# A hybrid decoder step: residual copy behind the token scaling, softmax bias from a minimum, sample probabilities a slot later

## The chip, the cores and the metric

The kernel runs on one core of one Trainium2 chip. The metric is the device time of one execution in microseconds (us); three runs are given, and their median is the time. One more execution was taken by the hardware profiler, and the rows of the profile come from it. Engines are named as the profile names them: PE is TensorE (matrix products and transposes), DVE is VectorE, ACT is ScalarE, POOL is GpSimd, SP is SyncE, which only issues transfers here.

## The reference

One layer of a decoder over a prompt of 1024 tokens and a sample group of 8 tokens (width 1024) that share the weights. A combined projection `w_in` feeds three mixers, whose outputs are gated, summed and merged; a SwiGLU follows. Cut to what the change touches:

```python
xn = rmsnorm(x, norm_mix_w)                       # the opening
sc_b, sc_c, sc_x, z, xbc, dt_raw, q, gates = split(xn @ w_in)
...
# mixer C: 4 heads of width 256 attend to 256 memory tokens
scores = einsum('blhd,bmhd->bhlm', q, mem_k) * (256 ** -0.5)     # 1/16
probs  = softmax(scores, axis=-1)
y_c    = einsum('bhlm,bmhd->blhd', probs, mem_v) @ w_attn_o
...
x = x + merge(...)          # the residual needs x as well as xn
x = x + swiglu(rmsnorm(x))
```

The prompt's memory keys and values are computed from `mem_prompt`; those of the sample tokens come from a cache.

## The kernel before

All matrix products run as split products: each fp32 operand is cut into a hi part (a cast) and a lo part (the remainder), and three products hi·hi, lo·hi and hi·lo are summed. Tensors lie with features on the 128 partitions and tokens along the free axis; the 1032 tokens are the prompt's 1024 and the 8 of the sample. A tile framework allots the buffers, and its scheduler settles the order of the instructions on each engine from the order of the program, from buffers and from estimated durations, so that a moved line can move others.

The stages by time in the profile: the opening (0 to 65 us), the in-projection by Strassen products, the state-space scan with the q projection as filler between the chunks, the attention (about 1340 to 1580 us) in between the out-projections, the merge and the SwiGLU, and the last rows.

**The opening** goes by four groups g of 256 tokens (the last with 8 more). For each group the rows of x are squared and summed (`square`, L528, ACT) and turned into reciprocal roots (`rsqrt`, `root_of`; L99 to L104), which PE spreads over the partitions (tile `ps_rb`) and DVE copies to `rbc`. Then `tokens(g, ks)` takes two of the eight feature blocks k at a time (one at a time in the last group): PE transposes x into one PSUM bank `ps_xt` (L495); ACT copies the bank to `xt` (L513) and starts the transfer of it to memory as `xT_d`, the residual kept for later (L515, on ACT's own queue); and `to_xn` makes the normalised tokens for each block: DVE multiplies the bank by the weight and `rbc` into `xw` (L501), ACT casts the hi part `xnh` (L502), DVE subtracts for the lo part `xnl` (L503). The pool of these banks, shared by all small PSUM tiles, has two buffers. Between the tiles of group g PE makes the first two products (`first_products`, tiles `ps_B` and `ps_C`, L565 to L567) and the step sizes (`step_sizes`, `ps_dt`, L575, L581) of group g - 1. Casts of the weights for the gemms that follow (`wz0h` by ACT, L152, `wz0l` by DVE, L153) stand among this work.

**The q projection**: `q_step` evicts each of eight blocks of q from PSUM by an ACT copy (L805), GpSimd copies the 8 sample columns to `qs`, and the block is stored to `q_d`.

**The attention** is cut into `pieces`, a list of slots each of which holds a few function calls; a pacing counter runs a slot or two after each of the out-projection's gemm steps. For each head h and each pair l2 of 128-token blocks, `a_scores` (L1647 to L1649, tile `psa`) makes the scores, `softmax` the probabilities: DVE takes the maximum (L1564) and multiplies it by -1/16 (L1565), ACT takes exp(score/16 + bias) with the sum (L1567), and DVE divides (L1571, L1573). `a_probs` (tile `psp`) transposes them and splits them, `a_out` (tile `psv`, copy to `ot` L1682) multiplies by the values. The sample tokens have pieces of their own: `s_query`, `s_keys`, `s_scores` (products of `qs` with the cached keys on DVE), then the list `late`: `s_softmax`, `s_values` (loads of cached values `vc`), `s_probs` (transposes into `pss_pT`, L1592), eight times `s_out` (`pso`, L1605), `s_back`. The weights `wo22r` and others are split among these pieces (L152, L153).

Of the kernel before, what the change touches and what calls it, by code (L numbers as in the profile page):

```python
# [11 lines left out]
AF = mybir.ActivationFunctionType  # L12
ALU = mybir.AluOpType
AX = mybir.AxisListType
# [12 lines left out]
KD = D // P  # L27
EPS = 1e-6
LAG = 3
GROUPS = 4  # L30
HEADS = 32
HPG = 8
# [9 lines left out]
def tile_kernel(ctx: ExitStack, tc, a, o):  # L42
    nc = tc.nc
    V, S, G, PE, SY = nc.vector, nc.scalar, nc.gpsimd, nc.tensor, nc.sync

    def f32(t):
        return t.bitcast(F32)
# [13 lines left out]
    def mm_ps(name):  # L61
        return pmm[0].tile([P, NCH, 512], F32, tag="mm", name=name)

    def sm_ps(name):
        return psm.tile([P, 512], F32, tag="sm", name=name)

    def dram(name, shape):
        return dp.tile(shape, F32, tag=name, name=name)
# [4 lines left out]
    def flat(ps):  # L73
        return ps[:, :, :CW]

    def t3(t, lo=0):
        return t[:, lo : lo + TT].rearrange("p (n c) -> p n c", n=NCH)
# [78 lines left out]
    def ev_tile(name, shape=(P, TT + 4), dt=F32):  # L156
        return ev.tile(list(shape), dt, tag="ev", name=name)
# [26 lines left out]
    def gemm(w, acts, name, width=P, off=0):  # L184

        hi, lo = w
        ps = mm_ps(name)
        nk = len(acts)
        n = int(pace[0] + pace[1])
        pace[1] += pace[0] - n  # L190
        marks = [nk * i // n for i in range(n)]
        between = seam.pop() if seam else None
        for k, (ah, al) in enumerate(acts):
            if between is not None:
                between(k)
            if k == 1 and owed:
                owed.pop()()
            for _ in range(marks.count(k)):
                tick()
            ks = slice(k * width + off, k * width + off + P)  # L200
            for i, (wt, x) in enumerate(((hi, ah), (hi, al), (lo, ah))):
                for n in range(NCH):
                    PE.matmul(  # L203
                        ps[:, n, :CW], wt[:, ks], x[:, n * CW : (n + 1) * CW],
                        start=(k == 0 and i == 0), stop=(k == nk - 1 and i == 2),
                    )
        return ps

    def wblock(w, col):
        return w[:, col : col + P].rearrange("(k p) c -> p k c", p=P)  # L210
# [10 lines left out]
    def b3(t, n):  # L221
        return t.rearrange("p (a b) -> p a b", a=n)

    def h3(t):
        return t.rearrange("p (n c) -> p n c", n=2)
# [16 lines left out]
    def st_ps(tag, name):  # L242
        return pst[0].tile([P, 2, 512], F32, tag=tag, name=name)
# [153 lines left out]
    v_d = dram("v_d", [2, P, D])  # L397
    ac_d = dram("ac_d", [GROUPS, NCK, HPG, P])
    ea_d = dram("ea_d", [GROUPS, NCK, HPG, P])
    bc_d = dram("bc_d", [GROUPS, NS, 2, P])  # L400
    qs_d = dram("qs_d", [NS, D])
# [21 lines left out]
    with tc.tile_pool(name="p0", bufs=1) as p0:  # L423
# [20 lines left out]
        ps = sm_ps("ps_mix")  # L444
# [26 lines left out]
        def par(key, i):  # L471
            return prm[:, PC[key] + i : PC[key] + i + 1]

        bias = cn.tile([P, 1], F32, tag="bias", name="bias")
# [14 lines left out]
        def part(g):  # L489
            c0, n = parts[g]  # L490
            return slice(c0, c0 + n)

        def turn(g, ps, at, of):
            for i, (t, n) in enumerate(srcs[g]):
                PE.transpose(ps[:, at + i * P : at + i * P + n], of(i, t, n), ident[:n, :n])  # L495

        def to_xn(g, k, ps):
            hi, lo = xn[k]
            c = part(g)
            xc = xw[k][:, c]  # L500
            first = V.scalar_tensor_tensor(xc, ps, par("mix", k), rbc[:, c], op0=ALU.mult, op1=ALU.mult)  # L501
            ins = S.copy(hi[:, c], xc)  # L502
            V.tensor_sub(lo[:, c], xc, f32(hi)[:, c])  # L503
            return ins.ins, first.ins

        def tokens(g, ks):

            n = parts[g][1]
            ps = sm_ps(f"ps_xt{g}{ks[0]}")
            for i, k in enumerate(ks):  # L510
                turn(g, ps, i * n, lambda _, t, m: t[:, k * P : (k + 1) * P])
            xt = p0.tile([P, 512], F32, tag="xt", bufs=4, name=f"xt{g}{ks[0]}")
            S.copy(xt[:, : len(ks) * n], ps[:, : len(ks) * n])  # L513
            to = xT_d[ks[0] :: 4] if len(ks) > 1 else xT_d[ks[0] : ks[0] + 1]
            S.dma_start(to[:, :, part(g)].rearrange("k p t -> p k t"), b3(xt[:, : len(ks) * n], len(ks)))  # L515
            for i, k in enumerate(ks):
                ins = to_xn(g, k, ps[:, i * n : (i + 1) * n])
            return ins

        def square(g, i):  # L520
# [119 lines left out]
    ys = cn.tile([P, 16, NS], F32, tag="ys", name="ys")  # L640
    bcs = ch.tile([P, GROUPS, NS, 2], F32, tag="bcs", name="bcs")

# [17 lines left out]
    def dt_tiles():  # L660
        mx, u, z, z2, q = (pd_.tile([P, W], F32, tag=n, name=n) for n in ("mx", "u", "z", "z2", "q"))
        da = pd_.tile([P, 9, HEADS], F32, tag="da", name="da")
        ach = pd_.tile([P, NCK, HEADS], F32, tag="ach", name="ach")
        return mx, u, z, z2, q, da, ach
# [33 lines left out]
    def dt_rows():  # L698
        act_, eat_ = (pd_.tile([HEADS, T], F32, tag="wide", bufs=2, name=n) for n in ("acT", "eaT"))

        V.tensor_copy(
            ach.rearrange("p c (g w t) -> p (c g) w t", g=GROUPS, w=2),
            acum.rearrange("p c (g t w) -> p (c g) w t", g=GROUPS, w=2),
        )
# [36 lines left out]
    def proj(col, name):  # L741
        return gemm(weights(wblock(w_in, col), "w" + name), xn, "ps_" + name)
# [58 lines left out]
    def q_step(i):  # L801
        def s():
            ps = proj(C_Q + i * P, f"q{i}")
            t = ev_tile(f"q{i}")
            S.copy(t3(t), flat(ps))  # L805
            G.tensor_copy(qs[:, i, :], t[:, T:TT])
            S.dma_start(q_d[i], t[:, :TT])

        return [Step(wblock(w_in, C_Q + i * P), f"wq{i}", s)]
# [523 lines left out]
    mx, u, z, z2, q, da, ach = dt_tiles()  # L1333
# [126 lines left out]
    ins = ((sc_d, a["w_sc_out"][0]), (yb_d, a["w_ssm_out"][0, 0:D]), (yb_d[8:16], a["w_ssm_out"][0, D : 2 * D]), (at_d, None))  # L1460
# [56 lines left out]
    if True:  # L1517
# [40 lines left out]
                    )  # L1558

        def softmax(pr, src, n, npart, name):  # L1560
            mxs = at.tile([P, 4], F32, tag="mx", name="mx" + name)
            mx, sm = mxs[:, :2], mxs[:, 2:]
            sv = b3(src, n)
            V.tensor_reduce(mx[:npart, :n], sv, axis=AX.X, op=ALU.max)  # L1564
            ins = V.tensor_scalar(mx[:npart, :n], mx[:npart, :n], -1.0 / 16.0, None, op0=ALU.mult)  # L1565
            for i in range(n):
                S.activation(  # L1567
                    pr[:, i, :], sv[:, i, :], AF.Exp, scale=1.0 / 16.0, bias=mx[:npart, i : i + 1],
                    accum_out=sm[:npart, i : i + 1],
                )  # L1570
            V.reciprocal(sm[:npart, :n], sm[:npart, :n])  # L1571
            for i in range(n):
                V.tensor_scalar(pr[:, i, :], pr[:, i, :], sm[:npart, i : i + 1], None, op0=ALU.mult)  # L1573
            return ins.ins
# [3 lines left out]
        def s_softmax():  # L1578
            ps = sm_ps("pss_sc")
            for m in range(2):  # L1580
                PE.transpose(
                    ps[:32, m * P : (m + 1) * P], sc_s[:, m].rearrange("p b h -> p (b h)"), ident
                )
            pr = ev_tile("prs", (P, MEM)).unsqueeze(1)[:32]
            softmax(pr, ps[:32, :MEM], 1, 32, "s")
            s_hold["pr"] = pr
# [99 lines left out]
        for h in range(AH):  # L1686
            for l2 in range(LAG + 4):
                late = [(a_probs, h, l2 - LAG)] if l2 >= LAG else []
                pieces.append(late + ([(a_scores, h, l2)] if l2 < 4 else []))
# [13 lines left out]
                pieces[at_].extend(fs)  # L1703
                at_ += 1
        at_ += 1
        late = [[(s_softmax,), (s_values, 0)], [], [(s_probs,)], []]
        for b in range(NS):
            late += [[(s_out, b)], [(states[b],)] if b < 4 else []]
        late += [[], [(s_back,)]]
# [28 lines left out]
    for m in range(KD):  # L1738
# [9 lines left out]
        ps = gemm(w, acts, f"po3{m}")  # L1748
# [59 lines left out]
    for half in range(2):  # L1808
        sq = ev_tile(f"sq{half}")
        for m in range(KD):  # L1810
# [3 lines left out]
            ps = mm_ps(f"pm{half}{m}")  # L1814
            for k, (ah, al) in enumerate(mg):
                if k in (0, 3, 6):
                    tick()
                ks = slice(k * P, (k + 1) * P)
# [8 lines left out]
            t = x2[m][:, HS[half]]  # L1827
# [171 lines left out]
    for part, js in enumerate(([0], [9, 10])):  # L1999
# [9 lines left out]
        for m in range(KD):  # L2009
            if not part:  # L2010
                x2[m] = big(f"x3_{m}")
            for half in range(2):
                ps = st_ps(tags[(2 * m + half) % 3], f"pd{part}{m}{half}")
                for k, (ah, al) in enumerate(hl):
                    ks = slice(k * cols + m * P % cols, k * cols + m * P % cols + P)
# [7 lines left out]
                t = h3(x2[m][:, HS[half]])  # L2023
# [123 lines left out]
    for n3, (c0, c1, tiles) in enumerate(  # L2147
# [3 lines left out]
        for m0 in range(0, KD, 3):  # L2151
            ms = range(m0, min(m0 + 3, KD))
            ps = mm_ps(f"pl{n3}{m0}")
            for k, (ah, al) in enumerate(hl):
                for m in ms:
                    wh, wl = wd[m // 2]
                    pb = ps[:, m - m0, :w]
                    ks = slice(k * 256 + (m % 2) * P, k * 256 + (m % 2) * P + P)
# [43 lines left out]
```

## Time and profile before

| what | value |
|---|---|
| runs | 2475.41, 2468.22, 2473.3 us |
| median | 2473.3 us |
| the profiled execution, by the clock of the runs | 2469.34 us |
| its span in the profile | 2467.3 us |
| mean granted TensorE clock | 0.999 |
| opening, until the first gemm | 64.86 us |

A row of the timeline gives start, duration, engine, line, operation, tiles (out <- in), shape and count; in brackets stands how long the engine was idle before it and what ended that. A row of the waits gives the waiting operation, what it waited for, the total, the number of times and the longest. A group gives the count, then busy time and mean nanoseconds of one, then the idle time ahead. The granted clock is the share of full speed that the throttle gave TensorE.

### The profile page before, as it was taken

What the parts mean: (1) busy time and instruction counts of PE and PEld (TensorE: products, weight loads), DVE (VectorE), ACT (ScalarE), POOL (GpSimd) and SP (SyncE); (2) the same over time, 40 slices, a digit from 0 to 9 for tenths busy, and PEclk for the clock granted to TensorE, in tenths of its full rate; (3) what the DMA queues carried; (4) which work ended last, traced back from release to release, by engine and by line L of the source; (5) the groups of instructions that cost most, each with busy time, mean ns of one, the idle gap of its engine ahead of it and who ended that gap; (6) DMA issues with size and microseconds to landing.
All of it is one profiled execution on the core that took longest, in us unless ns stands there. A gap on an engine that the chain in (4) does not pass through costs nothing. (4 is left out here: it accounts for less than half of the span.)

```text
span 2467.3 us, 45822 instructions
## 1 busy us (share of the span) xinstructions
PE 2428.0 (98%) x19020; PEld 2363.6 (96%) x19020; DVE 1602.1 (65%) x2606; ACT 1084.9 (44%) x1747; POOL 112.7 (5%) x163
## 2 busy tenths in 40 slices
PE   7999999999999999999999999999999999999998
PEld 5999999999999999898998998999999999999998
DVE  6844677777777675568677763554777555567855
ACT  6644554445453543656555442213443333343423
POOL 0100000000000000212211000000000000000000
PEclk9999999999999999999999999999999999999999
DMA  5445423444353345767886896855444333254522
GB/s 194 138 150 161 126 88 113 136 139 129 103 159 113 102 133 168 227 222 249 271 276 213 276 321 224 285 186 163 145 153 129 103 91 112 82 188 144 184 87 77
DMA packets 359608, 404.83 MB, mean 164 GB/s; under 512 B 16111, under 2 KB 286047, under 8 KB 359392
## 3 DMA queue, kind: packets, MB, share of 16 engines
q1 hardware_dynamic: 334374, 339.69, 44.4%
q10 hardware_dynamic: 25025, 62.21, 6.6%
q8 instruction: 150, 2.46, 0.4%
q14 instruction: 59, 0.48, 0.1%
HBM read 286.74 MB, written 115.32 MB: 163 GB/s over the span
## 5 line engine op out<-in xcount | busy, mean ns | idle before, releaser
L966 ACT ACTIVATE r<-r,acum 128x128 f32<-128x128 f32 x256 | 79.2, 392 | 4.2 <-DMA r<-ac_d 3.4
L756 DVE SCALAR_TENSOR_TENSOR ax<-u,prm,ax 128x1024 f32<-128x1024 f32 x44 | 56.4, 1282 | 0.1
L907 ACT ACTIVATE st<-st,es 128x128 f32<-128x128 f32 x128 | 41.2, 392 | 24.3 <-DMA st<-in_state_ssm_dram 19.4
L998 POOL TENSOR_TENSOR xdd<-xdt,decst 128x512 f32<-128x512 f32 x32 | 37.0, 1158 | 289.7 <-DVE xdt L994 289.7
L909 DVE SCALAR_TENSOR_TENSOR st<-sr,dts,st 128x128 f32<-128x128 f32 x128 | 40.6, 352 | 0.4
L992 DVE TENSOR_TENSOR r<-r,cbm 128x1024 f32<-128x1024 f32 x32 | 39.2, 1224 | 2.2
L1017 DVE TENSOR_TENSOR y<-po,ea 128x512 f32<-128x512 f32 x28 | 19.3, 688 | 28.1 <-PE po L1013 25.3
L913 DVE SCALAR_TENSOR_TENSOR sr<-st,sr 128x128 f32<-128x128 f32 x128 | 35.9, 291 | 1.1
L1454 DVE TENSOR_TENSOR yr<-po,yr 128x1032 f32<-128x1032 f32 x8 | 9.8, 1229 | 39.2 <-PE po L203 39.2
L1021 PE MATMUL py<-r,xdt 128*64 128x128 f32 x512 | 35.0, 279 | 0.0
L1828 DVE TENSOR_TENSOR x<-pm,xT 128x516 f32<-128x516 f32 x16 | 11.1, 696 | 36.3 <-PE pm L1821 36.2
L1034 PE MATMUL pss<-xdd,bT 128*128 128x512 f32 x64 | 34.2, 616 | 0.5 <-ACT bT L991 0.5
L967 ACT ACTIVATE r<-r 128x1024 f32<-128x1024 f32 x32 | 33.9, 1059 | 0.7
L1047 POOL TENSOR_TENSOR s<-s,cdec 128x512 f32<-128x512 f32 x28 | 33.1, 1181 | 2.5 <-DVE s L1040 2.3
L991 ACT COPY bT<-bp 128x128 f32<-128x128 f32 x32 | 8.5, 265 | 53.5 <-DVE cbm L989 53.5
L1750 DVE TENSOR_TENSOR gt<-po,gt 128x1032 f32<-128x1032 f32 x8 | 9.9, 1233 | 33.7 <-PE po L203 33.7
L1021 PEld LDWEIGHTS py<-r,xdt 128*64 128x64 f32 x512 | 27.3, 136 | 4.2 <-issue 0.9
L1013 PE MATMUL po<-bc,s 128*128 128x128 f32 x224 | 29.9, 276 | 0.0
L1013 PEld LDWEIGHTS po<-bc,s 128*128 128x128 f32 x224 | 28.2, 191 | 0.7 <-DVE s L1040 0.5
L759 DVE SCALAR_TENSOR_TENSOR ax<-u,prm,ax 128x1032 f32<-128x1032 f32 x22 | 28.4, 1290 | 0.0
L753 ACT ACTIVATE ax<-u,prm 128x1024 f32<-128x1024 f32 x22 | 27.4, 1246 | 1.4 <-DVE u L366 0.4
L1158 DVE SCALAR_TENSOR_TENSOR x<-x,prm,sqa 128x1032 f32<-128x1032 f32 x16 | 19.6, 1289 | 12.2 <-ACT sqa L1154 12.2
(9219 smaller groups left out, 9115.4 us busy)
## 6 DMA issues: line engine op xcount, KB each, us to landing
r<-ac_d SPq DMA_DIRECT2D x32, 512.0 KB
gt_d<-G ACTq DMA_DIRECT2D x24, 516.0 KB
gt<-gt_d SPq DMA_DIRECT2D x24, 516.0 KB
xs_d<-ax ACTq DMA_DIRECT2D x22, 516.0 KB
x<-xs_d SPq DMA_DIRECT2D x16, 516.0 KB
zs<-zs_d SPq DMA_DIRECT2D x16, 516.0 KB
yb_d<-x SPq DMA_DIRECT2D x16, 516.0 KB
in<-yb_d SPq DMA_DIRECT2D x16, 516.0 KB
```

The source lines that it names most:

```text
L756: V.scalar_tensor_tensor(acc[:, :T], u[:, j : j + T], w[j], acc[:, :T], op0=ALU.mult, op1=ALU.add)
L907: S.activation(st[:, i], st[:, i], AF.Copy, scale=es[:, g * 4 + i, b : b + 1])
L909: V.scalar_tensor_tensor(st[:, i], rb, dts[:, g * 4 + i, b : b + 1], st[:, i], op0=ALU.mult, op1=ALU.add)
L913: V.scalar_tensor_tensor(rb, st[:, i], 1.0, rc, op0=ALU.mult, op1=ALU.mult, accum_out=ys[:, g * 4 + i, b : b + 1],)
L966: S.activation(r[:, j, :], r[:, j, :], AF.Relu, scale=-1.0, bias=acum[:, c, h : h + 1])
L967: S.activation(r, r, AF.Exp, scale=-1.0)
L992: V.tensor_tensor(r, r, bc(cbm.unsqueeze(1), [P, HPG, P]), op=ALU.mult)
L998: G.tensor_tensor(b3(xdd, HPG), b3(xdt, HPG), bc(decst[:, c, hs].unsqueeze(2), [P, HPG, 64]), op=ALU.mult)
L1013: PE.matmul(po[:, t * P : (t + 1) * P], state["s"][:, t * P : (t + 1) * P], bcg[1][:, cs], start=True, stop=True,)
L1021: PE.matmul(py[hp : hp + 64, (h // 2) * P : (h // 2 + 1) * P], xdt[:, h * 64 : (h + 1) * 64], r[:, (h % 2) * 4 + h // 2, :], start=True, s ...
L1034: PE.matmul(pss, bT, xdd, start=True, stop=True)
L1047: G.tensor_tensor(b3(s_new, HPG), b3(state["s"], HPG), bc(cdec[:, c, hs].unsqueeze(2), [P, HPG, 64]), op=ALU.mult,)
```

## The change

Three edits. In `tokens`, both scalings of a tile, with their hi casts and lo subtractions, are issued ahead of the copy to `xt` and its transfer. For the softmax, q is multiplied by `QS` = -1/16 as it is evicted, by an ACT activation Copy in place of the plain copy; the scores then come out negated and scaled, the minimum over them is the bias as it stands, the exponential takes scale -1, and the scalar multiplication (17 instructions: 16 for the prompt, 1 for the sample) is gone. The sample's scores get the factor through `qs`. In `late`, `s_probs` is one slot later, which puts it right ahead of `s_out(0)` instead of a slot before that.

In the order of the instructions this moves, apart from the lines themselves: in the opening, ACT's order in each tile becomes two hi casts, copy, square; in the third group the casts of `wz0` come behind the last tokens' hi and lo parts instead of ahead of them; the C products of each group's last block now stand ahead of the next group's roots on PE. In the attention, the split of `wo22` comes ahead of the score tile's reduction, and `pss_pT` follows the score tile `psa3_0` on PE. The queue of SP has two weight loads and one load of keys a few places earlier; GpSimd's order is the same. The instruction counts are otherwise equal.

```diff
+QS = -1.0 / 16.0
...
@@ tokens(g, ks)
             for i, k in enumerate(ks):
                 turn(g, ps, i * n, lambda _, t, m: t[:, k * P : (k + 1) * P])
+            for i, k in enumerate(ks):
+                ins = to_xn(g, k, ps[:, i * n : (i + 1) * n])
             xt = p0.tile([P, 512], F32, tag="xt", bufs=4, name=f"xt{g}{ks[0]}")
             S.copy(xt[:, : len(ks) * n], ps[:, : len(ks) * n])
             to = xT_d[ks[0] :: 4] if len(ks) > 1 else xT_d[ks[0] : ks[0] + 1]
             S.dma_start(to[:, :, part(g)].rearrange("k p t -> p k t"), b3(xt[:, : len(ks) * n], len(ks)))
-            for i, k in enumerate(ks):
-                ins = to_xn(g, k, ps[:, i * n : (i + 1) * n])
             return ins
...
@@ q_step
-            S.copy(t3(t), flat(ps))
+            S.activation(t3(t), flat(ps), AF.Copy, scale=QS)
...
@@ softmax
-            V.tensor_reduce(mx[:npart, :n], sv, axis=AX.X, op=ALU.max)
-            ins = V.tensor_scalar(mx[:npart, :n], mx[:npart, :n], -1.0 / 16.0, None, op0=ALU.mult)
+            ins = V.tensor_reduce(mx[:npart, :n], sv, axis=AX.X, op=ALU.min)
             for i in range(n):
                 S.activation(
-                    pr[:, i, :], sv[:, i, :], AF.Exp, scale=1.0 / 16.0, bias=mx[:npart, i : i + 1],
+                    pr[:, i, :], sv[:, i, :], AF.Exp, scale=-1.0, bias=mx[:npart, i : i + 1],
                     accum_out=sm[:npart, i : i + 1],
                 )
...
-        late = [[(s_softmax,), (s_values, 0)], [], [(s_probs,)], []]
+        late = [[(s_softmax,), (s_values, 0)], [], [], [(s_probs,)]]
```

## The prediction

> **What bounds the kernel now.** I read the head of the page first, then the stretches by window.
>
> ```profile
> span 2467.3 us, 45822 instructions
> ...
> PE 2428.0 (98%) x19020; PEld 2363.6 (96%) x19020; DVE 1602.1 (65%) x2606; ACT 1084.9 (44%) x1747; POOL 112.7 (5%) x163
> ```
>
> TensorE (PE) is busy for all but 39 us of the span. The change adds and removes no TensorE work, so it can save only idle time of PE or time at a lower clock, and it can lose only by new idle time. It touches two stretches: the opening (until the gemms begin at 64.86 us) and the attention (1340 to 1580 us). The windows of the opening, from separate answers; in the first two the columns are window, length, PE busy with its count, granted clock, DMA share, GB/s; the third lists each engine in turn and ends with the clock, 0.91, and the DMA share and GB/s.
>
> ```profile
> 0.00:70.00 70.00, 54.67 (x390) 0.98 0.60 195
> 46.00:52.00 6.00, 5.70 (x39) 0.72 0.41 113
> 46.42:64.86 18.44, 18.14 (x146) 13.36 (x144) 11.97 (x25) 11.47 (x27) 1.60 (x1) 0.91 0.36 109
> ```
>
> The opening leaves PE idle for 70.00 - 54.67 = 15.3 us, and it holds a stretch at a granted clock of 0.72: 6.00 x (1 - 0.72) = 1.7 us of full-speed work lost. Behind 46.42 us PE is idle for only 0.3 us; there the opening is bound by PE. What PE waited for in the first 70 us (time in total, times, longest):
>
> ```profile
> PE ps_B L565 <- ACT xnh L502: 4.0, 5, 1.7
> ...
> PE ps_B L566 <- DVE xnl L503: 1.5, 3, 0.8
> PE ps_xt L495 <- ACT xnh L502: 1.0, 2, 0.8
> ```
>
> So 5.5 us are waits for the turned and scaled tokens (hi part by ScalarE, ACT; lo part by VectorE, DVE), and 1.0 us waits for a PSUM bank to come free. These are the terms that the first edit reaches.
>
> **Edit 1: scale ahead of the copy (opening).** PE's timeline, third token group (g = 2) from its row of root factors to the end:
>
> ```profile
> 31.67 0.38 PE L495 MATMUL ps_rb<-ident,rst 128*128 128x128 f32 x2
> ...
> 39.34 0.63 PE L495 MATMUL ps_xt<-ident,x 128*128 128x128 f32 x4 [0.82 <-ACT xnh L502]
> ...
> 44.21 0.39 PE L565 MATMUL ps_B<-xnh,wB0h 128*128 128x256 f32 x1 [0.97 <-ACT xnh L502]
> ...
> 45.50 0.39 PE L566 MATMUL ps_B<-xnl,wB0h 128*128 128x256 f32 x1 [0.79 <-DVE xnl L503]
> 45.72 0.28 PE L567 MATMUL ps_B<-xnh,wl 128*128 128x256 f32 x1
> 45.84 0.28 PE L566 MATMUL ps_C<-xnl,wC0h 128*128 128x256 f32 x1
> ...
> 46.42 0.53 PE L495 MATMUL ps_rb<-ident,rst 128*128 128x128 f32 x3
> ...
> 51.73 0.39 PE L565 MATMUL ps_B<-xnh,wB0h 128*128 128x264 f32 x1 [0.30 <-ACT xnh L502]
> ```
>
> Products follow each other by 0.12 us (45.72 to 45.84) though each is shown at 0.28. ACT's and DVE's timelines beside it (of DVE the first row; its other two belong to edit 2):
>
> ```profile
> 32.52 0.59 ACT L513 COPY xt<-ps_xt 128x512 f32<-128x512 f32 x1 [2.31 <-PE ps_xt L495]
> ...
> 36.67 1.05 ACT L528 ACTIVATE junk<-x 128x1024 f32<-128x1024 f32 x1
> ...
> 42.82 1.03 ACT L152 CAST wz0h<-wz0r 128x1024 fp32r<-128x1024 f32 x1
> 42.84 0.37 ACTq L515 DMA_DIRECT2D xT_d<-xt  x1
> 43.76 0.71 ACT L502 CAST xnh<-xw 128x256 fp32r<-128x256 f32 x2
> ```
>
> ```profile
> 33.14 0.88 DVE L501 SCALAR_TENSOR_TENSOR xw<-ps_xt,prm,rbc 128x256 f32<-128x256 f32 x2 [0.63 <-ACT xt L513]
> ...
> 1448.82 1.22 DVE L153 TENSOR_TENSOR wo22l<-wo22r,wo22h 128x1024 fp32r<-128x1024 f32 x1
> 1449.95 0.17 DVE L1565 TENSOR_SCALAR mx<-mx 128x2 f32<-128x2 f32 x1
> ```
>
> The copy at 32.52 is that of group 1's last tile. The first scale starts at 33.14, 0.03 after the copy's end at 32.52 + 0.59 = 33.11: of one bank, the scales wait for the copy. After the change the copy waits for the scales, and ACT's order becomes two hi casts, copy, then the square of the next group. Nothing is removed; for each tile the scaled tokens come up to 0.59 + 0.03 = 0.62 us earlier, and the copy with its DMA issue (0.37, on ACT's own queue) stands behind them. [...]
>
> Groups 0 and 1: the chain to the next group's root runs through ACT's squares, and these stay behind the same copies. I take the one 0.62 of the first tile as the gain up to group 2's ps_rb (31.67 becomes 31.05); ends 0 and 1.2, for none and for two such tiles.
>
> Group 2: ACT's square at 36.67 comes to 36.3 (0.62 earlier, less 0.25, an estimate, by which the copies in front now follow casts). From there: square 1.05, casts 0.7, copy 0.59, square 1.05, casts 0.6, copy 0.59 end at about 40.75. That last copy frees the bank for the fourth tile's transposes, which start then instead of at 39.34 and wait some 1.9 us, not 0.82. Behind them PE has 4 transposes (0.47) and five parts of six products (5 x 0.72 = 3.6), plus one wait for a lo part, which I put at 0.5, a little under the 0.79 shown: the root row comes at 40.75 + 0.47 + 3.6 + 0.5 = 45.3 instead of 46.42, with three C products (0.36) already done that now follow it. So 1.1 + 0.36 = 1.5 us are won. The waits of 0.97 and 0.79 go because the weight cast wz0h at 42.82 (1.03) now stands behind the last hi casts, which it delayed at 43.76; the weight isn't needed before 64.86, which hides it.
>
> Group 3: PE waits less just ahead of 46 us, so I take the clock to stay up: +1.7. Its eight tiles have banks that come free later by some 0.45 (the copy now follows scales of 0.88 and casts instead of preceding the scales). PE's other work, mostly the products of the group before, covers this but for one place like the 0.30 at 51.73: -0.3. Opening: 1.5 + 1.7 - 0.3 = 2.9 us. Ends: 1.5 - 0.3 = 1.2, if the slow clock stays or moves, and 2.9 + 0.6 + 0.3 = 3.8, if two tiles gain ahead of group 2 and the release costs nothing.
>
> **Edit 2: the prompt softmax.** The groups by line and form (busy, mean ns of one, idle before):
>
> ```profile
> L805 ACT COPY q<-ps_q 128x1032 f32<-128x1032 f32 x8 | 8.1, 1012 | 0.0
> L841 ACT ACTIVATE z<-ps_z 128x1032 f32<-128x1032 f32 x2 | 2.1, 1032 | 5.1 <-PE ps_z L203 5.1
> L1565 DVE TENSOR_SCALAR mx<-mx 128x2 f32<-128x2 f32 x16 | 2.7, 168 | 0.4
> ```
>
> The scaled eviction of q isn't in the trace; its nearest row is L841, an activation of the same shape: 8 x (1032 - 1012) = 0.16 us on ACT, which is 44% busy. Hidden by double PSUM buffers; uncovered it would cost 0.16, and a gain has no reason. A minimum reduces as many elements as the maximum; I take the same time. Removing the scalar op saves 0.17 between scores and exponential, 16 times (and once in the sample's), but counts only where PE waits for the probabilities. PE's waits, 1450 to 1580 us:
>
> ```profile
> PE psa L1647 <- ACT pr L1567: 2.4, 2, 1.6
> PE pss_pT L1592 <- ACT ot L1682: 1.0, 1, 1.0
> PE pcs L1505 <- ACT ot L1682: 0.9, 1, 0.9
> ```
>
> Only two of the score tiles wait. For the first (1.6) the DVE row at 1448.82 says why: the weight subtraction wo22l, 1.22, came between the reduction and the scalar op at 1449.95. With no scalar op it can't; the scheduler puts it ahead of the reduction instead, where the delay is nearly the same: 0.15 won. The second (0.8): 0.35, for two scalar ops. Sum 0.5; ends 0 and 2.4.
>
> **Edit 3: the sample's probabilities one slot later.** s_probs' two transposes waited 1.0 us for a bank that an output copy (ot) held. A slot later they stand behind the next scores and that copy is done: 1.0 won. Nothing is pushed back, since s_out already follows in the same slot as before, but it now reads pTs sooner after its copy, for which I keep 0.4 at the low end: 0.6. What is late next is the 0.9 (pcs), which stays. Attention: 0.5 + 1.0 = 1.5 us, ends 0.6 and 3.4.
>
> **The sum.** 2.9 + 1.5 = 4.4 us, ends 1.8 and 7.2. The profiled execution took 2469.34 us by the clock of the runs (2 us more than its span): 2469.34 - 4.4 = 2464.9. It lies 4.0 below the median 2473.3, so on the median's scale the forecast is 2473.3 - 4.4 = 2468.9, with 2466.1 to 2471.5 as its own range. The three runs spread over 7.2 us (2468.22 to 2475.41), and 0.3%, about what a measurement of this kernel can tell from no change, is 7.4 us.
>
> **The rivals.**
>
> *More than that.* The clock stays up, two tiles gain in groups 0 and 1, both psa waits vanish because the score tiles now stand elsewhere among the weight splits, and the pcs wait of 0.9 goes with the changed slot: 3.8 + 3.4 + 0.9 = 8.1, so 2465.2; with further waits for hi parts out of the 4.0 gone it reaches 2461. For it: all these waits come from an order on ACT and DVE that changes here. Against: each of them must go in full. Chance 0.28.
>
> *The clock falls elsewhere.* The slow stretch at 46 to 52 us follows waits of 0.97 and 0.79 within 2 us. In the new order PE waits 1.9 us at one place, near 39 us. If the clock drops behind that, the 1.7 is lost there instead: 4.4 - 1.7 = 2.7 won, 2470.6. For it: 1.9 is as much idling as 0.97 + 0.79 = 1.76, which went ahead of the slow stretch. Against it: group 1 had a single wait of 1.7 (the longest in the row of L565), and the whole of the first 70 us lost 70 x (1 - 0.98) = 1.4, no more than the slow stretch alone, so that wait cost no clock. Chance 0.17. [...]
>
> *Slower: the banks come free too late.* The two banks of this pool are taken in turn by every transpose tile, and each is now held some 0.45 us longer. If PE reaches its transposes within 0.45 us of the release at all 20 tiles (12 in groups 0 to 2, 8 in group 3), that is 20 x 0.45 = 9.0, less 1.5 in the attention: 7.5 lost, 2480.8. It decides from the point where PE has less than 0.45 us of other work between taking a bank and needing it back. Against it: before, PE waited for a bank twice in the whole opening (1.0 us). For it: group 3 is PE-bound, with one part a tile and so little between its transposes. Chance 0.10.
>
> *Nothing.* The opening's gain runs into a wait for the next weights at 64.86 and the softmax is hidden: 2473.3. Chance 0.05; DMA is busy for 0.36 before that point, so the weights are there.
>
> **How the numbers follow.** Forecast 0.40, then 0.28, 0.17, 0.10, 0.05. Faster by over 0.3%: most of the first rival and, by the scatter of a median, a part of the forecast: 0.24 + 0.12 = 0.36. Slower: 0.10. Within: 0.54. The range goes down to 2461, the first rival's far end, and up to 2476, which holds the forecast, the falling clock, no change and its scatter of some 3 us; the slower rival lies outside.
>
> **What would show it right or wrong.** Right: in the new profile group 3's first product at about 48.8 us instead of 51.73, the gemms starting at about 62 instead of 64.86; a granted clock near 1 from 46 to 52; one bank wait of about 1.9 ahead of group 2's last transposes; the wait for ot at L1592 (now two lines on) gone; PE's busy time the same but for the clock's 1.7. Wrong: several new waits of ps_xt for xt copies with 0.4 to 0.5 us each (the slower rival), a clock below 0.8 between 38 and 46, or a psa wait larger than 2.4.

## The result, and the profile after

The changed kernel takes 2462.11 us (median of 7 runs, 2460.18 to 2468.11) against 2471.15 (7 runs, 2468.22 to 2475.41) of the kernel before on the same chip: ratio 0.9965, 95% interval 0.9952 to 0.9979. A second set on another chip gave 0.9967 (0.9955 to 0.9980). So it is faster by 8 to 9 us, about twice the 4.4 that were forecast.

The two profiled executions lie only 4.6 us apart (2469.34 and 2464.70), which is less than the medians do; the reason comes below. Head of the page, and the windows of the opening (columns as before):

```profile
span 2463.0 us, 45791 instructions
...
PE 2426.6 (99%) x19020; PEld 2363.1 (96%) x19020; DVE 1599.3 (65%) x2589; ACT 1084.4 (44%) x1747; POOL 107.4 (4%) x163
```

```profile
46.00:52.00 6.00, 5.49 (x39) 4.58 (x38) 3.94 (x10) 3.88 (x11) 0.00 (x0) 1.00 0.57 176
...
0.00:70.00 70.00, 58.28 (x420) 49.00 (x421) 49.18 (x127) 46.14 (x100) 1.68 (x11) 1.00 0.61 195
```

The granted clock from 46 to 52 us is 1.00 instead of 0.72, and PE is busy 3.6 us longer within the first 70 us (58.28 against 54.67): it has got further. PE's waits there, and its timeline (line numbers two higher than before):

```profile
PE ps_B L567 <- ACT xnh L504: 1.9, 4, 0.6
PE ps_B L568 <- DVE xnl L505: 0.7, 3, 0.4
```

```profile
30.67 0.38 PE L497 MATMUL ps_rb<-ident,rst 128*128 128x128 f32 x2
...
38.69 0.60 PE L497 MATMUL ps_xt<-ident,x 128*128 128x128 f32 x4
...
43.54 0.55 PE L497 MATMUL ps_rb<-ident,rst 128*128 128x128 f32 x3
...
46.81 0.39 PE L567 MATMUL ps_B<-xnh,wB0h 128*128 128x264 f32 x1 [0.51 <-ACT xnh L504]
```

The waits for hi and lo parts fall from 5.5 to 2.6 us. The third group's root row comes at 30.67 (31.67 before), the fourth's at 43.54 (46.42), group 3's first product at 46.81 (51.73), and the gemms begin at 60.56 instead of 64.86. The transposes of group 2's last tile at 38.69 carry no wait. ACT's timeline of the third group shows why:

```profile
37.65 0.58 ACT L517 COPY xt<-ps_xt 128x512 f32<-128x512 f32 x1
...
39.78 0.59 ACT L517 COPY xt<-ps_xt 128x512 f32<-128x512 f32 x1
...
41.31 0.69 ACT L504 CAST xnh<-xw 128x256 fp32r<-128x256 f32 x2
41.91 0.57 ACT L517 COPY xt<-ps_xt 128x512 f32<-128x512 f32 x1
42.39 0.20 ACT L102 ACTIVATE rs_t<-rs_v 128x3 f32<-128x3 f32 x1
42.50 1.03 ACT L154 CAST wz0h<-wz0r 128x1024 fp32r<-128x1024 f32 x1
```

The copy at 37.65 is that of the group's second tile and the one at 39.78 that of its third. The fourth tile's transposes take the second tile's bank, free at 38.23, before PE comes. The last casts stand at 41.31 (43.76 before), ahead of wz0h. PE's waits in the attention, 1340 to 1580 us:

```profile
PE psa L1649 <- ACT pr L1569: 3.1, 2, 2.6
PE pcs L1507 <- ACT ot L1684: 1.6, 1, 1.6
PE psp L1663 <- DVE pTl L1671: 1.6, 2, 1.0
```

The wait of the sample's transposes (1.0) is gone, but the three above have grown from 2.4, 0.9 and 0.6. In this execution the attention gained nothing; set beside the one before, instruction by instruction, the lead is 4.30 us at the gemms, 3.1 at 1300 us, 2.8 at 1600 and 4.3 at the end.

### The profile page after: what moved, and what is told of

The parts are those of the page before. It is cut to its first block, busy times and chain, and to the rows that moved or that the text cites. A ratio compares the mean times of both kernels' runs of the same rounds, so it can differ in the third digit from the quotient of the medians.

```text
span 2463.0 us, 45791 instructions
## 1 busy us (share of the span) xinstructions
PE 2426.6 (99%) x19020; PEld 2363.1 (96%) x19020; DVE 1599.3 (65%) x2589; ACT 1084.4 (44%) x1747; POOL 107.4 (4%) x163
## 4 chain that ended last, share of the span: by engine, by line
PE 85%; DMA 6%; DVE 5%; ACT 3%; issue 1%; SPq 0%; DVEq 0%; ACTq 0%; POOL 0%
PE po L205 11%; PE pm L1823 4%; PE ps_q L205 3%; PE pss L1036 1%; PE py L1023 1%; DMA qb<-qs_d 1%; PE ps_z L205 1%; PE po L1015 1%; DMA in<-yb_d 1%; PE G16m L253 1%; PE Z14m L253 1%; PE Z2m L253 1%; PE d00m L253 1%; PE d16m L253 1%; PE d14m L253 1%
## 5 line engine op out<-in xcount | busy, mean ns | idle before, releaser
L1557 DVE SCALAR_TENSOR_TENSOR kc<-kc,qb 128x256 f32<-128x256 f32 x64 | 23.7, 421 | 9.7 <-DMA qb<-qs_d 8.3
```

## The experiments

**The edits one by one.** Each kernel is the one before with only the parts of the diff that its label names; all figures are means or medians against the runs of the kernel before on the same chip.

> Only the first edit (scales and casts ahead of the residual copy), the attention as before. Theory A (the gain is the opening's, the attention gives nothing): the gemms begin at about 60.6 us as in the changed kernel (64.86 before), clock 1.00 from 46 to 52 us, and the time is all of the change's: 4 to 9 us less than before, ratio 0.9965 to 0.998. Theory B (the attention edits carry the 4.7 us that the profiled pair doesn't show): 4.3 less, ratio 0.9983, and the other two edits give as much again.

> Only the second edit (scaled q, minimum as the bias). Theory A: within 1.5 us of before (ratio 0.9994 to 1.0006); the waits of the score tiles stay at about 2.4 to 3.1 us in all, since the weight splits on VectorE still stand between scores and bias; opening as before, 64.9 us to the gemms. Theory B: 2 to 3 us less.

> Only the third edit (sample probabilities a slot later). Theory A: the wait of 1.0 us of the sample's transposes for an output copy goes, and 0.3 to 1.0 us of it is left at the end of the attention; ratio 0.9996 to 1.0. Theory B: 2 us less.

> The second and third edits, the opening as before. Theory A: the attention's waits are those of the changed kernel (6 to 7 us in all against 6 before) and the time is within 1.5 us of before, ratio 0.9994 to 1.0006. Theory B: 4 to 5 us less, ratio 0.998. With the first edit alone this tells whether the parts add up to 9.0.

Then, on a second and a third chip, the whole change again and the first edit with either of the others:

> The changed kernel once more, as the measure for the others of this call. The single edits gave 2.0, 2.8 and 2.2 us by their means (first alone, second alone, third alone), second and third together 1.9, all with intervals of about 2.2; in the whole set a run's time goes with its mean granted clock, some 2.5 us for each 0.001. Theory A (parts add up, and the 9.0 of the first seven runs was helped by a higher clock, 0.9989 against 0.9978): 4 to 6 us less than before, ratio 0.9976 to 0.9984. Theory B (the edits help each other): 8 to 9 us less, ratio 0.9964 to 0.9968, at equal clock too.

> First and third edit, the softmax as before. Theory A (the softmax edit gives nothing of its own): as fast as the whole change within 1.5 us. Theory B (it takes part): 2 to 3 us slower than the whole change. The wait of the sample's transposes is gone in both; the score tiles wait 2 to 3.3 us in all.

> First and second edit, the slot as before. Theory A (the third edit carries the attention's gain: the transposes' wait for an output copy is 1.0 to 2.6 us in every profile without it and absent with it): 3 to 5 us slower than the whole change, about 2466.5, with that wait back at 1 to 2.6 us. Theory B (the softmax edit carries it): within 1.5 us of the whole change, and the score tiles' waits well below the 2.4 of before.

And the first edit alone a second time:

> The first edit alone once more. In its first set it was 2.0 us under before by the means, though its opening is 2.8 to 4.3 us shorter, while the first edit with the third gave 7.0 and with the second 7.4. Theory A (without an attention edit the earlier start runs into longer waits at the score tile and the sample's transposes, which are followed by a stretch at half clock): again 1 to 3.5 us under before, ratio 0.9986 to 0.9996, with a wait of the score tiles of over 3 us or a clock under 0.7 in the attention. Theory B (the first set was chance; the first edit gives its 2.8 us and what it saves in slow clock at 46 us): 3.5 to 5 us under before, ratio 0.998 to 0.9986, and no stretch of slow clock in the attention.

| edits | median us | before | ratio, 95% interval | mean less by, us | mean clock (before) |
|---|---|---|---|---|---|
| 1 | 2469.26 | 2471.10 | 0.9993 (0.9985 to 1.0002) | 2.0 | 0.9980 (0.9978) |
| 1, again | 2467.67 | 2470.60 | 0.9991 (0.9982 to 1.0000) | 2.5 | 0.9981 (0.9979) |
| 2 | 2467.57 | 2471.10 | 0.9992 (0.9984 to 1.0001) | 2.8 | 0.9987 (0.9978) |
| 3 | 2467.78 | 2471.10 | 0.9995 (0.9985 to 1.0005) | 2.2 | 0.9979 (0.9978) |
| 2 + 3 | 2468.31 | 2471.10 | 0.9992 (0.9983 to 1.0002) | 1.9 | 0.9982 (0.9978) |
| 1 + 3 | 2464.46 | 2471.02 | 0.9971 (0.9962 to 0.9981) | 7.0 | 0.9986 (0.9974) |
| 1 + 2 | 2465.08 | 2472.73 | 0.9969 (0.9956 to 0.9981) | 7.4 | 0.9988 (0.9976) |
| 1 + 2 + 3 | 2462.11 | 2471.15 | 0.9965 (0.9952 to 0.9979) | 8.5 | 0.9989 |
| 1 + 2 + 3, again | 2462.95 | 2471.02 | 0.9967 (0.9955 to 0.9980) | 8.5 | 0.9986 (0.9974) |

The first four rows were measured on one chip, the first edit's second set on another, and the pairs on a third and a fourth. The first edit alone is worth 2 to 2.5 us, in two sets on two chips; the attention edits alone are worth 2 to 3 us, singly or together. Each of these has an interval of about 2 us to either side, and the ratios' intervals all reach to 1, so they decide little between the theories above: the first edit has the opening of its theory A (gemms at 60.57 us, clock 1.00) but half of the gain that either theory asked for; the softmax and the slot alone come out as their theories B by the means; both together lie 0.4 us outside theory A. With the first edit, either of the others gives 7, and with both it is 8.5, where the parts make 2.2 + 1.9 = 4.1. The excess of 4.4 has an interval of about 3 us to either side, worked out from the spread of the runs, so it is clear of zero; the excess of the pairs (2.6 with the slot, 2.4 with the softmax) is not, with as wide an interval. Theory A expected 4 to 6 for the whole and fell; theory B, that the edits help each other, expected 8 to 9 and holds in the time, but not at the equal clock that it named (0.9986 against 0.9974). Of the two theories on the attention neither came true alone: with the first edit, either of the others comes within 1 to 1.5 us of the whole change. The first edit's second set came out as its theory A in the time (2.5); its score tile waited 2.0 us, not over 3, and a stretch at half clock followed, as shown below.

**What each part does in the profile.** The opening is the same in all kernels that have the first edit (root rows at 30.5 to 30.7 and 43.35 to 43.54), so it can be read exactly. The sample's transposes waited for the output copy in every profile without the third edit, 1.0 to 2.6 us, and never with it. The first edit alone (first row, its second set), the softmax alone (second row):

```profile
PE pss_pT L1592 <- ACT ot L1682: 1.5, 1, 1.5
```

```profile
PE pss_pT L1592 <- ACT ot L1682: 2.1, 1, 2.1
PE pcs L1506 <- ACT ot L1682: 1.3, 1, 1.3
PE psa L1647 <- ACT pr L1567: 1.0, 2, 0.5
```

The score tiles waited 1.8 to 3.3 us in all without the softmax edit and 1.0 to 3.1 with it (1.0, 1.4, 1.8, 2.3, 3.1; 1.4 in the kernel with VectorE's copies below): a little less on the whole, with an overlap.

**The slow clock.** The time of a run goes with its mean granted clock. Of the 35 runs of the kernel before on the first of these chips, the two at 0.996 took 2474.0 us on the mean, the ten at 0.997 took 2473.1, the sixteen at 0.998 took 2470.2 and the seven at 0.999 took 2467.7. The profiles show what lies behind: single stretches at a clock of 0.5 (in the first edit alone it was 0.50 for all of 1450 to 1455 us). In the clock's record in the trace each is 3.41 us long, one of them 6.83 (but for the one at the record's end, 6.07 us from 2463.58 on before and 5.95 from 2459.06 on after), so 3.41 x 0.5 = 1.7 us are lost, at a few places that differ from execution to execution. In each profile the stretches start a whole number of these lengths apart (in the kernel before once more at 45.23, 304.65 and 1485.66 us: 76 and 346 times 3.413). The opening before appears unchanged in five profiles. Windows from 46 to 52 us of the softmax alone, the slot alone, both together, and the kernel before once more:

```profile
46.00:52.00 6.00, 5.77 (x37) 3.10 (x36) 1.66 (x4) 3.32 (x7) 0.00 (x0) 0.72 0.38 110
```

```profile
46.00:52.00 6.00, 5.77 (x48) 3.93 (x47) 2.81 (x8) 4.08 (x9) 0.00 (x0) 1.00 0.46 136
```

```profile
46.00:52.00 6.00, 5.77 (x46) 3.74 (x45) 3.04 (x8) 4.49 (x11) 0.00 (x0) 1.00 0.50 153
```

```profile
46.00:52.00 6.00, 5.76 (x39) 3.45 (x38) 1.70 (x5) 3.33 (x7) 0.00 (x0) 0.78 0.36 107
```

> The kernel before, one more profile. Theory A (the slow clock stretch at 46 to 52 us is a matter of chance in its opening: seen in two of the four profiles with that opening): either the granted clock is 0.7 and the gemms begin at 64.9, or it is 1.00 and they begin at 63.4 us; nothing in between. Theory B (it belongs to the order before): 0.7 again. The transposes of the sample wait 1 to 2.6 us for the output copy either way.

It came slow (0.78, gemms at 64.39 us), which either theory allows; what speaks for theory A are the two siblings of the same order that did not, and both of these were known before this run. With the profile before that is three slow of five. The two that stayed at 1.00 both have the third edit and the three others lack it; it changes no instruction of the opening, but five profiles can't show that this is chance. From the first root row (at 8.5 to 8.8 us, behind the loads of the first rows of x) to the gemms the opening takes 55.8 to 56.2 us with the slow stretch (before, the softmax alone, before once more) and 54.1 to 54.9 without (both attention edits, the slot alone). With the first edit it takes 51.7 to 52.0, and the clock was 1.00 in all profiles that have it. So the first edit saves about 2.6 us at full clock, and 1.5 more in executions in which the old order draws the slow stretch.

The same thing happens in the attention, from 1445 to 1460 us. The windows of the first edit alone (both sets), with the slot, with the softmax, and of the whole change:

```profile
1445.00:1460.00 15.00, 11.72 (x65) 11.43 (x64) 12.41 (x37) 7.25 (x19) 0.00 (x0) 0.77 0.93 320
```

```profile
1445.00:1460.00 15.00, 12.84 (x79) 12.28 (x78) 13.65 (x43) 6.71 (x20) 0.00 (x0) 0.89 1.01 348
```

```profile
1445.00:1460.00 15.00, 13.21 (x83) 12.71 (x81) 13.02 (x38) 7.84 (x19) 0.00 (x0) 0.89 0.89 303
```

```profile
1445.00:1460.00 15.00, 12.68 (x82) 12.39 (x81) 12.56 (x34) 8.63 (x20) 0.00 (x0) 0.89 0.97 344
```

```profile
1445.00:1460.00 15.00, 11.26 (x79) 10.48 (x77) 13.30 (x37) 7.87 (x19) 0.00 (x0) 1.00 0.98 342
```

All four that have the first edit without both others lose clock there: 15 x (1 - 0.77) = 3.5 us, and 15 x (1 - 0.89) = 1.7 in three. Each of these stretches begins in or behind one wait of a score tile, of 3.27, 1.95, 1.79 and 2.32 us. The whole change's profile has a wait of 2.58 us at the same tile, ending at 1450.24, and the kernel before once more one of 2.05, ending at 1453.04, both at a clock of 1.00. What tells them apart is where the wait falls in the steps of 3.41 us, counted from the start of each clock record (in the profile before the stretch begins 30.72 us, 9.00 of them, behind it): a border at 1448.72 cuts the 2.58 into 1.06 and 1.52, one at 1451.53 the 2.05 into 0.54 and 1.51. In the four with a stretch 1.79 us or more of the wait lie within one step, in the ten other profiles 1.57 or less. This is worked out from the traces after the fact; no run was made to test it. The repetition lost 1.7 at 1170 us and 1.7 at 1340 us instead.

**Why the opening is shorter.** Two kernels take the first edit apart. In the first, the kernel before holds back only the cast of the first gemm weight:

```diff
-        in_turn("hi", S.copy(hi, raw))
+        with tc.issue_after(held[0]) if name == "wz0" else nullcontext():   # held: last cast of group 2
+            in_turn("hi", S.copy(hi, raw))
```

> Before, with one thing changed: the cast of the first gemm weight (wz0h) is held back behind the last hi cast of the third group, so that its lo part on VectorE comes behind that group's last lo part too. Theory A (this displacement is about 1.2 us of the opening's gain): the row of roots ps_rb of the last group comes at 45.2 to 45.4 us instead of 46.42, and the waits of 0.97 and 0.79 at 44 to 46 us shrink to under 0.7 in all. Theory B (it is all the earlier scaling): 46.2 to 46.4. Measured at ps_rb, since the slow clock that follows it in some executions shifts what is later.

```profile
31.36 0.38 PE L497 MATMUL ps_rb<-ident,rst 128*128 128x128 f32 x2
...
44.77 0.55 PE L497 MATMUL ps_rb<-ident,rst 128*128 128x128 f32 x3
...
61.85 0.74 PE L205 MATMUL ps_z<-xnh,wz0h 128*128 128x344 f32 x3
```

From one root row to the next it takes 13.41 us, against 46.42 - 31.67 = 14.75 before and 12.87 after. That is theory A, a little more than it expected, and of the waits of 0.97 and 0.79 one of 0.58 is left. But the rows do not stand at the same places among PE's first products: 57 of these lie between the two rows here, 59 before and 60 after. At 0.12 us each, this kernel gains 1.34 - 0.24 = 1.1 us and the change 1.88 + 0.12 = 2.0. From the third root row to the gemms it takes 30.49 us here, 31.7 in the two unchanged openings at full clock, and 29.89 after, where two products fewer (0.24) are left to do. So 1.2 of 1.6 us come with the place of one weight cast, not with the scaling as such. In the second, the scales stand ahead of the copy, but the casts stay behind it:

```diff
 for i, k in enumerate(ks):
-    ins = to_xn(g, k, ps[...])          # scale, hi cast, lo
+    first = to_xn(g, k, ps[...])        # scale only
 S.copy(xt, ps); S.dma_start(...)
+for k in ks:
+    ins = to_hl(g, k)                   # hi cast, lo
```

> Before, with the scales ahead of the copy but the hi casts behind it: VectorE's scale no longer waits for the copy, yet the copy (0.59 us) still stands between the scales and the casts on ScalarE. Here too the scheduler puts wz0h behind the last hi cast. Theory A (what counts is when the casts come): the first hi cast of a tile is 0 to 0.4 us later than before, and ps_rb of the third and fourth group comes no earlier than 31.3 and 45.0 us. Theory B (the scale's wait for the copy was the limit): nearly the changed kernel's, 30.7 and 43.5 us.

```profile
30.93 0.40 PE L495 MATMUL ps_rb<-ident,rst 128*128 128x128 f32 x2
...
44.89 0.55 PE L495 MATMUL ps_rb<-ident,rst 128*128 128x128 f32 x3
...
61.67 0.74 PE L203 MATMUL ps_z<-xnh,wz0h 128*128 128x344 f32 x3
```

The third group takes 13.96 us, 0.8 less than before, with 60 products between the rows (so 0.9 gained), and from the third root row to the gemms it is 30.74, with the two products fewer: 0.7 of the 1.6 us. wz0h stands behind the casts here as well, and that place alone gave 1.2: with the casts late, part of it is lost again. The row at 44.89 is 0.1 short of theory A's 45.0 and far from 43.5. For the row at 30.93 neither is right; it lies between the two, and the rows of the five unchanged openings (31.15 to 31.79) spread as widely as the difference. So it counts when the casts come, in the third group, as far as one profile of each kernel shows; the first two groups stay undecided.

**A further version.**

```diff
+eng = V.tensor_copy if g < 3 and ks[0] < len(srcs[g + 1]) else S.copy
-S.copy(xt, ps)
+eng(xt, ps)
```

> The changed kernel, with the residual copy on VectorE instead of ScalarE in those tiles that carry a square of the next group (two a group, three in the third). Theory A (in the changed opening ScalarE sets the pace: per tile casts 0.7, copy 0.58, square 1.05 against TensorE's 1.9): the rows of roots come 0.4 to 1.2 us earlier than the changed kernel's 30.67 and 43.54, and the gemms at 59.4 to 60.2 instead of 60.56; the time is 0.5 to 1.2 us under the changed kernel's, less than these rounds can tell. Theory B (the waits left are VectorE's or the transposes'): no earlier, or later by up to 1 us, since VectorE now copies between scale and lo part.

```profile
30.78 0.40 PE L497 MATMUL ps_rb<-ident,rst 128*128 128x128 f32 x2
...
43.74 0.55 PE L497 MATMUL ps_rb<-ident,rst 128*128 128x128 f32 x3
...
60.76 0.74 PE L205 MATMUL ps_z<-xnh,wz0h 128*128 128x344 f32 x3
```

Nothing is earlier, although ScalarE is relieved of seven copies: theory B. The time is 2462.88 us against 2472.73, ratio 0.9962 (0.9949 to 0.9975), which can't be told from the whole change. That ScalarE's busy time sets the pace is not borne out; but VectorE took the copies over, so the run can't exclude that a gain on one engine and a loss on the other cancel.

## Why the prediction was right or wrong

The direction, the likeliest stage and the mechanism in the opening were right, and the measured times lie in the range near its low end. But 8 to 9 us are twice the 4.4 that were forecast, and the forecast's own range (2466.1 to 2471.5) does not hold the times: that the whole range does is owed to the room left for the first rival. Point by point:

- **Groups 0 and 1.** One tile's 0.62 us was forecast. From the first to the third root row it takes 22.0 us after, and 22.4 to 23.2 in the five unchanged openings: 0.4 to 1.2, about 0.8, and two products (0.24) more lie ahead of that row. So it is about 1.0, within the ends of 0 and 1.2.
- **Group 2, the step that failed.** Its own gain was put at 1.12 - 0.62 + 0.36 = 0.86 us (the terms up to the copy, as listed, end at 40.88, not 40.75); by the root rows it is 14.75 - 12.87 = 1.88, with 0.36 more for the three products moved ahead of its last row and 0.24 less for the two moved ahead of its first, so 2.0. The failing term is the bank wait of 1.9 us: the prediction had the fourth tile's transposes wait for the third tile's copy. The pool has two banks, and between two tiles no other tile takes one here, so they wait for the second tile's copy, over at 38.23, and PE came at 38.69. The price of that mistake is about 1.1 us.
- **The weight cast.** That the waits of 0.97 and 0.79 go because wz0h moves was right: in the kernel that moves it alone 0.58 of them is left, and 1.2 us are won by the gemms. That the place behind the last casts is free ("which hides it") was wrong, as the next point shows.
- **Group 3.** Without the slow stretch it takes 16.93 us from its root row to the gemms in two unchanged openings and 17.02 after, with 0.36 less work: about 0.45 lost, where 0.3 was forecast. The size is near, the cause another. No wait for an `xt` copy stands there, and so the slower rival's mechanism is not seen. On DVE the lo part of the weight, `wz0l`, now stands in front of the copy of the root factors, which starts 1.16 us behind its row instead of 0.57:

```profile
43.56 1.23 DVE L155 TENSOR_TENSOR wz0l<-wz0r,wz0h 128x1024 fp32r<-128x1024 f32 x1 [0.17 <-ACT wz0h L154]
44.70 0.43 DVE L538 COPY rbc<-ps_rb 128x264 f32<-128x264 f32 x1
```

  The bank of `ps_rb` comes free with this copy at 45.13, the next transposes start at 45.19, and group 3's first product waits 0.51 us for its hi part (0.16 in the two unchanged openings). This is read from the rows; no run changes it alone.
- **The clock.** The stretch is gone, as forecast, and where the forecast put 1.7 us on every execution it costs 1.5 in three of five. The rival in which the clock falls behind a wait near 39 us had no such wait to start from. Its counter-argument, that the wait of 1.7 cost no clock, is not shown: that wait ends at 12.73 us, but the clock's record begins only at 16.2 us, and the windows count what lies ahead of it as full speed. Products follow each other there by 0.21 us (14.61 to 14.82) instead of 0.12; in the profile after they do too (13.58 to 13.79), where the wait at that place is 0.41, so the slow pace can't be put down to the 1.7 either. What the traces show of when the clock falls is little: stretches that start a whole number of 3.41 us apart, the same opening slow in three profiles and not in two others, and 1.76 us of waits, in two, ahead of the stretch in the profile before.
- **The opening in all.** 2.9 us were forecast. It is 2.6 at full clock and 4.30 in the profiled pair. The sum came near by luck, by errors against each other: 1.1 too little in group 2 and 0.4 in groups 0 and 1, and a clock term of 1.7 counted in full.
- **The attention.** 1.5 us were forecast. Alone the two edits gave 1.9 (an interval of about 2 to either side), which agrees but would agree with nothing as well. The wait of the transposes went as forecast, and was 1.0 to 2.6 us in other executions, so 1.0 was low. That the score tiles' wait would stay because wo22l only changes places with the scalar operation was right in kind, but not its gain of 0.5: in the profile after it grew to 3.1, the longest 2.6. A wait larger than 2.4 was to be a sign of being wrong; the time fell all the same.
- **What the sum left out.** It had no term for what the edits do to each other, and this is half of the effect: 8.5 us against 4.1 for the parts. Part of it goes with the clock: the mean clock rose by 0.0002 with the first edit, by 0.0004 with the other two and by 0.0011 with all three, and 0.0005 x 2470 = 1.2 us. What lies behind that clock, and the other 3 us, no run here assigns to a wait: the profiles of the pairs lose clock at 1450 us as those of the first edit alone do. It stays open. The first rival (8.1 us, 2465.2) came nearest, but for a reason it named only in part.
- **The profiled pair.** Its 4.6 us are a draw from two spreads: the runs of one kernel lie up to 10 us apart, in part by how many slow stretches each has: of the spread of the 35 runs, the mean clock accounts for somewhat over half (0.58 of the variance).

## What to carry to other kernels

Where several readers take turns on one PSUM bank, put the one on the path first (VectorE's scales waited for ScalarE's copy 9 times, 9.2 us in all, in the profile before), and then look at what the scheduler does with the work that no longer fits in front: here most of what the third and fourth groups gained (1.2 of 1.6 us) came with a weight cast that fell behind the last tokens. Before a wait for a buffer is priced, count the buffers through and name the reader that frees the one in question. When the effect is a few microseconds, compare rows of the trace from a common mark, since times of whole runs scatter with the granted clock by more than that (the 35 runs of the kernel before by 10.0 us), and measure the edits together as well as apart.

## What the runs showed that was not expected

Stretches at half clock, 3.41 us long and 1.7 us dear, come at the same few places in a kernel that is otherwise 98% busy: 45, 300, 1170, 1340, 1450 and 1485 us, each in some executions only. They go with a good part of the scatter of whole runs (2473.1, 2470.2 and 2467.7 us at mean clocks of 0.997, 0.998 and 0.999). In the profile before, the one at 46.94 us followed waits of 0.97 and 0.79 us, 1.76 within 4 us. At 300, 1170 and 1340 us no wait goes ahead at all, and PE is shown as busy throughout (with the first edit and the softmax, 5.00 of 5.00 us from 300 to 305 and from 1170 to 1175, at a clock of 0.66); what stands there are products of few columns, transposes of 8x8 at 300 us and at the other two places rows like this one, of the softmax alone, ahead of its stretch at 1175.82 us:

```profile
1172.57 2.14 PE L1135 MATMUL psny<-ones,sqa 128*128 128x1 f32 x18
```

The same products stand in every kernel here, most often without such a stretch. What sets the clock back at these places no run here shows.
